# One level of Strassen for the down projection, with weight sums made in DRAM by accumulating transfers

## The chip, the cores and the metric

The program runs on one core of a Trainium2 chip. The metric is the device time of one execution in microseconds, taken as the median of several runs. A profile is one further look at an execution: it lists every instruction of each engine with its start and duration, and the DMA traffic. Engines are named as the profile names them: PE is TensorE, PEld its weight loads, DVE is VectorE, ACT is ScalarE, POOL is GpSimd, SP is SyncE (here it only issues DMAs).

## The reference

One decoder layer on 512 tokens of width 2048, in float32. It is a token mixer (gated linear attention, HGRN2 and latent attention head groups with one input and one output projection) followed by a SwiGLU feed-forward network of inner width 5632. Only the last line of the network is changed:

```python
x = x + rms_norm(m, attn_post_norm[l])
u = rms_norm(x, ffn_pre_norm[l])
f = (jax.nn.silu(u @ w_gate[l]) * (u @ w_up[l])) @ w_down[l]
x = x + rms_norm(f, ffn_post_norm[l])
```

Here `silu(...) * (...)` is 512 x 5632, called h below, and `w_down` is 5632 x 2048.

## The kernel before

Each float32 product is made of three matmuls. An operand is split into a high part, rounded to the type fp32r, and a low part, the remainder: `whi` (ACT, line 100) and `wlo` (DVE, line 107) split a weight tile, `split` (lines 128 and 129) an activation. `mm3` then issues high times high, high times low and low times high into one PSUM accumulator.

The stages follow one another. The mixer reads its weights as tiles of 128 x 1024 (512 KB) through `wsplit`: SP issues the load, ACT and DVE split it, PE works 24 matmuls of 512 columns on it. The tags `ws` (raw), `wh` and `wl` (split) have three buffers each, so SP runs a few tiles ahead of PE and waits until a buffer comes free. The first loops are `first_blocks` (eight tiles: four steps over the width of x, two blocks each) and two further blocks in `gemm_fm` (eight tiles). A scheduler that runs when the kernel is built sets the order of the instructions on each engine here; what a queue then does first is fixed.

After that `bridge` writes the order out by hand for PE, DVE, ACT and POOL: a list of `items` (a source tile, and the product that uses it), and dictionaries `pre_`, `post` and `tops` of functions that are called at an item's index. It contains the output projection, the norms, and gate and up. Gate and up already use one level of Strassen's scheme (Winograd's form, 7 products in place of 8): the weight differences are made by DVE (`tdiff`, line 1024). The first 24 of 44 units have two of their products done ahead (`NPRE`), and there POOL makes 256 of 1024 columns of the low part (line 109). SP's order is still the scheduler's.

`down` (line 1185) is the last stage. h has been written to DRAM by `hout` (`hd`, 44 tiles of 128 x 512). For each of two halves p of the output columns and each of 44 tiles k it loads one weight tile `wd[p, k]`, splits it and the h tile, and issues 24 matmuls of 512 columns (4 token groups x 2 column blocks x 3) into eight PSUM accumulators, 2 x 44 x 24 = 2112 in all:

```python
for tt in range(NTT):
    for c in range(2):
        self.mm3(ps[tt][c], hh[:, ts], hl[:, ts], wh[:, cs], wl[:, cs], k == 0, k == FT - 1)
```

The last six tiles of the second half are ordered by token group, so that three of the four groups are finished (squares, norm, residual, output) while PE still works.

## Time and profile before

| | |
|---|---|
| three timed runs | 2244.81, 2245.75 and 2250.26 us, median 2245.75 us |
| span of the profiled execution | 2249.2 us, 35218 instructions |
| PE busy | 2213.9 us, 98% |
| DVE / ACT / POOL busy | 1457.8 / 911.3 / 254.0 us |
| DMA moved | 299.86 MB, mean 133 GB/s |
| down projection | from about 1760 us to the end |

The span runs from the first to the last instruction; the profile gives no other time for that execution, and its span lies within the three timed runs. A row of a timeline gives the start, the duration, the engine, the line of the kernel, the operation, and what is written and read; in brackets is how long the engine was idle before it and what ended that. Matmuls overlap, so their pace is read from the distance of the starts and not from the duration.

### The profile page before, as it was taken

Reading aid. Unit: us, or ns where it says so; the run is one execution under the profiler, and the core shown is the slowest. Engines: PE = TensorE matmul, PEld = TensorE weight load, DVE = VectorE, ACT = ScalarE, POOL = GpSimd, SP = SyncE. Lnnn points to the kernel's source line nnn. Section 1 sums busy time; section 2 is a strip of 40 time slices with the busy share of each in tenths; the row PEclk is TensorE's granted clock in tenths of the full one; section 3 lists DMA queues with packets and bytes.
Section 4 is the critical chain, followed back from the end, with each engine's and each line's share of the span. In section 5 each row is a group of like instructions: output and inputs, shape, how many; then the busy total and the mean of one; then the engine's idle time right before and its main releaser. Section 6 shows DMA issues by size and latency. Waiting matters only on the chain.

```text
span 2249.2 us, 35218 instructions
## 1 busy us (share of the span) xinstructions
PE 2213.9 (98%) x14150; PEld 2005.5 (89%) x14150; DVE 1457.8 (65%) x2238; ACT 911.3 (41%) x1274; POOL 254.0 (11%) x218
## 2 busy tenths in 40 slices
PE   9999999999999999999999999999999999999998
PEld 7878887888879999999999999999999888888886
DVE  6347777535554577897888778999999623343345
ACT  5324343336553444654444444444343422232231
POOL 2012311000001665530000000000000000000000
PEclk9999899999999999999999999999999999999999
DMA  6222112232103576884333343666655744433332
GB/s 206 93 85 66 57 57 62 94 95 83 66 29 103 183 221 196 251 259 129 118 118 114 119 125 122 186 203 207 188 181 171 253 141 123 130 94 95 102 103 104
DMA packets 108340, 299.86 MB, mean 133 GB/s; under 512 B 12160, under 2 KB 29328, under 8 KB 108176
## 3 DMA queue, kind: packets, MB, share of 16 engines
q1 hardware_dynamic: 105152, 292.10, 41.6%
q10 hardware_dynamic: 3024, 5.51, 0.7%
q8 instruction: 111, 1.82, 0.3%
q14 instruction: 53, 0.43, 0.1%
HBM read 271.34 MB, written 26.21 MB: 132 GB/s over the span
## 4 chain that ended last, share of the span: by engine, by line
PE 90%; DVE 5%; POOL 1%; ACT 1%; issue 1%; DMA 1%; SPq 0%; DVEq 0%; ACTq 0%; POOLq 0%
PE acc L120 18%; PE acc L122 18%; PE acc L121 18%; PE aux L122 10%; PE aux L120 10%; PE aux L121 10%; DVE wl L107 1%; PE aux L541 1%; PE aux L755 1%; DVE u L526 1%; ACT wh L100 0%; DVE u L955 0%; PE aux L588 0%; PE aux L723 0%; PE aux L741 0%
## 5 line engine op out<-in xcount | busy, mean ns | idle before, releaser
L120 PE MATMUL acc<-u,wh 128*128 128x256 f32 (+2 forms) x2064 | 635.0, 309 | 2.6 <-ACT wh L270 1.4
L121 PE MATMUL acc<-u,wh 128*128 128x256 f32 (+2 forms) x2064 | 635.7, 308 | 0.0
L122 PE MATMUL acc<-u,wl 128*128 128x256 f32 (+2 forms) x2064 | 634.6, 308 | 0.1
L107 DVE TENSOR_TENSOR wl<-ws,wh 128x1024 fp32r<-128x1024 f32 (+2 forms) x315 | 375.5, 1193 | 305.2 <-ACT wh L100 299.0
L100 ACT ACTIVATE wh<-ws 128x1024 fp32r<-128x1024 f32 (+1 forms) x315 | 329.9, 1049 | 498.9 <-PE acc L121 141.2
L120 PEld LDWEIGHTS acc<-u,wh 128*128 128x128 f32 (+1 forms) x2064 | 395.5, 192 | 21.4 <-ACT wh L270 1.9
L122 PEld LDWEIGHTS acc<-u,wl 128*128 128x128 f32 (+1 forms) x2064 | 395.4, 192 | 19.1 <-DVE wl L107 1.0
L121 PEld LDWEIGHTS acc<-u,wh 128*128 128x128 f32 (+1 forms) x2064 | 395.8, 192 | 17.9 <-DVE u L250 0.4
L122 PE MATMUL aux<-u,wl 128*128 128x256 f32 (+1 forms) x1264 | 362.3, 287 | 1.9 <-DVE wl L107 1.9
L120 PE MATMUL aux<-u,wh 128*128 128x256 f32 (+1 forms) x1264 | 362.8, 287 | 0.3 <-ACT wh L100 0.3
L121 PE MATMUL aux<-u,wh 128*128 128x256 f32 (+1 forms) x1264 | 362.1, 286 | 0.0
L100 ACT ACTIVATE wh<-wt 128x1024 fp32r<-128x1024 f32 x176 | 186.9, 1062 | 299.1 <-PE aux L121 112.8
L122 PEld LDWEIGHTS aux<-u,wl 128*128 128x128 f32 x1264 | 243.5, 193 | 3.8 <-DVE wl L107 2.5
L120 PEld LDWEIGHTS aux<-u,wh 128*128 128x128 f32 x1264 | 243.6, 193 | 1.8 <-ACT wh L100 0.5
L121 PEld LDWEIGHTS aux<-u,wh 128*128 128x128 f32 x1264 | 243.6, 193 | 1.2
L107 DVE TENSOR_TENSOR wl<-wt,wh 128x1024 fp32r<-128x1024 f32 x176 | 215.0, 1222 | 34.0 <-ACT wh L100 33.9
L120 PE MATMUL acc<-wh,u 128*128 128x512 f32 x356 | 140.2, 395 | 0.0
L121 PE MATMUL acc<-wl,u 128*128 128x512 f32 x356 | 140.1, 394 | 0.0
L122 PE MATMUL acc<-wh,u 128*128 128x512 f32 x356 | 139.5, 394 | 0.0
L120 PE MATMUL acc<-wh,m 128*128 128x512 f32 x260 | 101.1, 389 | 0.0
L121 PE MATMUL acc<-wl,m 128*128 128x512 f32 x260 | 101.1, 389 | 0.0
L122 PE MATMUL acc<-wh,m 128*128 128x512 f32 x260 | 101.1, 389 | 0.0
(293 smaller groups left out, 3037.2 us busy)
## 6 DMA issues: line engine op xcount, KB each, us to landing
ws<-wgu_in SPq DMA_DIRECT2D x136, 512.0 KB, 3.8
wsx<-wgu_in SPq DMA_DIRECT2D x88, 512.0 KB, 3.7
ws<-wd_in SPq DMA_DIRECT2D x88, 512.0 KB, 3.7
ws<-wo_in SPq DMA_DIRECT2D x56, 512.0 KB, 3.7
ws<-wf_in SPq DMA_DIRECT2D x39, 512.0 KB, 3.6
ws<-wt_in SPq DMA_DIRECT2D x32, 512.0 KB, 3.6
hd<-g SPq DMA_DIRECT2D x44, 256.0 KB, 2.8
u<-hd SPq DMA_DIRECT2D x30, 256.0 KB, 3.9
```

What stands on the lines that cost most here:

```text
L100: self.nc.scalar.activation(h, st, AF.Copy)
L107: nc.vector.tensor_tensor(lo[:, :d], st[:, :d], h[:, :d], op=ALU.subtract)
L120: mm(ps, lhsT=ah, rhs=bh, start=start, stop=False)
L121: mm(ps, lhsT=ah, rhs=bl, start=False, stop=False)
L122: mm(ps, lhsT=al, rhs=bh, start=False, stop=stop)
L526: nc.vector.tensor_tensor(qt[hs].rearrange("p (c h n s) -> p c h n s", c=NTT, h=2, s=s)[:, :, h], c3(v3(q)[:, :, 1, :]), c3(dv[:, :, 1, :] ...
L541: mm(ps[:m, c * 64:(c + 1) * 64], lhsT=kt[:, c * P:c * P + m], rhs=qt[:, c * 64:(c + 1) * 64], start=True, stop=True)
L755: mm(po[:, ts], lhsT=v[kt][:, (h % 4) * P:(h % 4 + 1) * P], rhs=pT[:, kt * P:(kt + 1) * P], start=kt == 0, stop=kt == tt)
```

## The change

The down projection becomes one level of the same seven-product scheme. The inner width is cut into 11 groups of four tiles ("duos"), the tokens into two halves, the output columns into two halves; each weight block is cut again into 512-column parts p. An item is one 128 x 1024 tile of a weight block or weight sum, and has 12 matmuls of 512 columns (2 token groups x 2 tiles x 3). There are 2 parts x 11 duos x 7 products = 154 items and 1848 matmuls.

The four sums of weight blocks (td, 11.5 MB each) are not made by an engine. `weight_sums` copies a block of `wd` into `td` in DRAM with eight plain transfers on SP's queue (1.44 MB each), and then adds another block with eight accumulating transfers on POOL's queue. There are 32 plain and 32 accumulating transfers: t1 and t3 are copied (16), both get b12 added (16), t2 is copied from t1 (8), gets b22 (8), t4 is copied from t2 (8), gets b21 (8). The program calls one step of it at every second weight tile of the mixer, 40 in all, and the other 24 at units of gate and up.

The sums of h blocks are made by DVE, products are gathered in two PSUM pairs that are evacuated after each product into 16 accumulators in SBUF, and the stage joins the hand-written list, so that its loads may begin seven items ahead. The last norm and the output are in `stat` and `final`.

```diff
--- before.py
+++ after.py
-NEXT = 22
...
+NROW = DFF * D // 4 // 2048
...
+    def weight_sums(self):
+        nc, t = self.nc, self.t
+        flat = lambda v: v.rearrange("a d p n -> (a d p n)").rearrange("(r n) -> r n", n=2048)
+        b11, b12, b21, b22 = (flat(t["wd"][q]) for q in range(4))
+        t1, t2, t3, t4 = (flat(t["td"][q]) for q in range(4))
+        for step in (((t1, b11, False), (t3, b22, False)), ((t1, b12, True), (t3, b12, True)),
+                     ((t2, t1, False),), ((t2, b22, True),), ((t4, t2, False),),
+                     ((t4, b21, True),)):
+            for dst, src, add in step:
+                for r in range(0, NROW, NROW // 8):
+                    d, v = dst[r:r + NROW // 8], src[r:r + NROW // 8]
+                    if add:
+                        nc.gpsimd.dma_start(d, v, accum_op=ALU.add, max_dma_last_dim=8192)
+                    else:
+                        nc.sync.dma_start(d, v)
+                    yield
+
     def wsplit(self, src, n=1024):
+        if self.bg is not None:
+            self.nbg += 1
+            if self.nbg % 2 == 0 and self.nbg <= 80:
+                next(self.bg, 0)
...
-        with tc.tile_pool(name="ext", bufs=NEXT, reuse_waits="tile") as self.M:
-            self.down()
...
         self.first_blocks(wf, scaled(hf))
+        self.bg = self.weight_sums()
...
+            at(pre_, i, lambda: next(self.bg, 0))
+        self.down_items(items, pre_, post, tops, at)
...
-    def down(self):
+    def down_items(self, items, pre_, post, tops, at):
         nc, t = self.nc, self.t
-        hs = []
-
-        def load(k):
-            h = self.u() if k < NHU else self.mx()
-            nc.sync.dma_start(h, t["hd"][k])
-            hs.append(h)
-
-        for k in range(4):
-            load(k)
-        gr, x2 = [], {}
-
-        def loads():
+        base = len(items)
+        duos = [NPRE + 4 * d for d in range((FT - NPRE) // 4)] + [4 * d for d in range(NPRE // 4)]
+        chunks = [duos[i:i + 2] for i in range(0, len(duos), 2)]
+        nchunk = len(chunks)
...
+        def sload(d):
+            r = raw[d] = {}
+            for n, e, hs in (("11", 0, 0), ("21", 0, 256), ("22", 1, 256), ("12", 1, 0)):
+                r[n] = self.u()
+                nc.sync.dma_start(
+                    r[n].rearrange("p (k s) -> p k s", k=2),
+                    t["hd"][d + e:d + 4:2].rearrange("k p s -> p k s")[:, :, hs:hs + 256])
+
+        def ssum13(d):
+            r = raw[d]
+            r["S1"] = self.u()
+            D.tensor_tensor(r["S1"], r["21"], r["22"], op=ALU.subtract)
+            D.tensor_tensor(r["21"], r["11"], r["21"], op=ALU.subtract)
+            r["S3"] = r.pop("21")
...
+        def conv(d, kind):
+            S[d, kind] = self.split(raw[d][KEY[kind]])
+        ORDER = (1, 5, 6, 3, 7, 2, 4)
...
+        def load(i, p, n, d):
+            tag = TAGS[i % 10]
...
+            q = SRC[n]
+            nc.sync.dma_start(st, (t["wd"][q] if q < 4 else t["td"][q - 4])[p, duos.index(d)])
...
+        def prod(c, p, n, d):
...
+                for tt in range(2):
+                    for j in range(2):
+                        a = slice(j * 256 + tt * P, j * 256 + (tt + 1) * P)
+                        w = slice(j * 512, (j + 1) * 512)
+                        mm = lambda l, r, st, sp: nc.tensor.matmul(
+                            ps[tt], lhsT=l[:, a], rhs=r[:, w], start=st, stop=sp,
+                            skip_group_check=True)
+                        mm(hi, wh, first and j == 0, False)
+                        mm(hi, wl, False, False)
+                        mm(lo, wh, False, last and j == 1)
...
+        def evac(c, p, n):
+            ps = bank[which(p, n)]
+            name, sign = EV[n]
+            for tt in range(2):
+                a = acc.get((p, name, tt))
+                if a is None:
+                    a = acc[p, name, tt] = self.u()
+                    nc.scalar.activation(a, ps[tt], AF.Copy, scale=float(sign))
+                elif sign > 0:
+                    D.tensor_tensor(a, a, ps[tt], op=ALU.add)
+                else:
+                    D.tensor_tensor(a, a, ps[tt], op=ALU.subtract)
...
+        def stat(p, name, tt, eng=None):
...
+            if name == "C11":
+                D.tensor_tensor(f, bank[p][tt], f, op=ALU.add)
+            sq = self.gv()
+            nc.scalar.activation(sq, f, AF.Square, accum_out=ssc[tok][:, cc:cc + 1])
+            (eng or D).tensor_tensor(f, f, gr[cc], op=ALU.mult)
+
+        def final(tok):
+            ss = self.sm(1)
+            D.reduce_sum(ss, ssc[tok], axis=mybir.AxisListType.X)
+            r = self.rstd(ss, D_, 1)
+            row, tt = tok // 2, tok % 2
+            for cc in range(4):
+                f = acc[cc % 2, f"C{row + 1}{cc // 2 + 1}", tt]
+                D.scalar_tensor_tensor(f, f, r, x2[tok, cc], op0=ALU.mult, op1=ALU.add)
+                nc.sync.dma_start(self.out[tok * P:(tok + 1) * P, cc * 512:(cc + 1) * 512], f)
...
+        for c, ds in enumerate(chunks):
+            for p in range(2):
+                b0 = len(items)
+                for o, n in enumerate(ORDER):
+                    for k, d in enumerate(ds):
+                        i = len(items)
+                        j = i - base
+                        at(pre_, max(base - 4, i - 7), load, j, p, n, d)
+                        items.append((lambda j=j: W.pop(j), prod(c, p, n, d), 0))
+                    if n in EV:
+                        at(pre_, len(items), evac, c, p, n)
...
+        for name, o in (("C12", -2), ("C22", -1), ("C11", 0)):
+            for tt in range(2):
+                at(pre_, end + o, stat, 1, name, tt)
+        for tok in (0, 1):
+            at(pre_, end, final, tok)
+        for tt in range(2):
+            at(pre_, end + 1, stat, 1, "C21", tt, D)
+        for tok in (2, 3):
+            at(pre_, end + 1, final, tok)
...
     a["wd"] = np.ascontiguousarray(
-        f["w_down"][0].reshape(FT, P, 2, 1024).transpose(2, 0, 1, 3))
+        f["w_down"][0].reshape(FT // 4, 2, 2, P, 2, 2, 512)[[k // 4 for k in order]]
+        .transpose(2, 4, 5, 0, 3, 1, 6)).reshape(4, 2, FT // 4, P, 1024)
...
+                     ("td", (4, 2, FT // 4, P, 1024))):
```

The order on SP after the 16 loads of x and the small constants, before the change. `ws_...` is a weight tile in the order of use; `ws_355` is the sixth of the sixteen tiles named above.

```order
L95 DMA ws_355<-wf_in 128x1024
L95 DMA ws_417<-wf_in 128x1024
L95 DMA ws_447<-wf_in 128x1024
L95 DMA ws_524<-wf_in 128x1024
L95 DMA ws_554<-wf_in 128x1024
L95 DMA ws_584<-wf_in 128x1024
L95 DMA ws_614<-wf_in 128x1024
L95 DMA ws_652<-wf_in 128x1024
L95 DMA ws_682<-wf_in 128x1024
```

The same place after the change (a tile may have another number: 555 is 554 before, 585 is 584, 616 is 614, 654 is 652, 685 is 682). `td<-wd_in` is a plain copy of 1.44 MB, `td<-td` one that reads a finished t1.

```order
L126 DMA td<-wd_in 32x11264 x2
L95 DMA ws_355<-wf_in 128x1024
L126 DMA td<-wd_in 32x11264 x5
L95 DMA ws_417<-wf_in 128x1024
L126 DMA td<-wd_in 32x11264 x4
L95 DMA ws_447<-wf_in 128x1024
L126 DMA td<-wd_in 32x11264 x5
L95 DMA ws_524<-wf_in 128x1024
...
L126 DMA td<-td 32x11264 x2
L95 DMA ws_616<-wf_in 128x1024
L126 DMA td<-td 32x11264 x5
L95 DMA ws_654<-wf_in 128x1024
L126 DMA td<-td 32x11264
L95 DMA ws_685<-wf_in 128x1024
```

All 24 plain copies of the mixer's share now stand among these eight loads, the first two ahead of `ws_355` and the last just ahead of `ws_685`, the fourteenth tile.

POOL before, behind its last sum of squares of x (`m_104`); line 515 is the decay product of the first head groups. In brackets are the counters that a row waits for.

```order
L258 TENSOR_TENSOR m_104<-m_104,m_361 128x512 [waits DVE_49,Activation_49]
L258 TENSOR_TENSOR m_104<-m_104,m_377 128x512 [waits DVE_49,Activation_49]
L515 TENSOR_TENSOR m_1084<-u_508,m_1086 128x512 [waits Activation_49,Pool_49]
L515 TENSOR_TENSOR m_1106<-u_510,m_1108 128x512 [waits Activation_49]
L515 TENSOR_TENSOR m_1085<-u_508,m_1121 128x512 [waits Activation_49]
```

POOL after the change at the same place. `DMAHW0` to `DMAHW7` count finished transfers of SP's queue, `DMASW0` to `DMASW7` those of POOL's; line 535 is line 515 of before.

```order
L277 TENSOR_TENSOR m_104<-m_104,m_377 128x512 [waits DVE_49,Activation_49]
L124 DMA td<-wd_in 176x2048 [waits DMAHW6_49]
L124 DMA td<-wd_in 176x2048 [waits DMAHW7_49]
...
L124 DMA td<-wd_in 176x2048 [waits DMAHW7_49]
L124 DMA td<-wd_in 176x2048 [waits DMAHW0_49,DMASW0_49]
...
L124 DMA td<-wd_in 176x2048 [waits DMAHW0_49,DMASW7_49]
L535 TENSOR_TENSOR m_1092<-u_508,m_1094 128x512 [waits Activation_49,Pool_49]
```

Each of the 16 accumulating transfers waits for the plain copy that it adds to, and the second eight also for the first eight. All of them now stand ahead of the head groups' work on POOL.

SP before, where gate and up reach the third of the full units; `ws` and `wsx` are its weight tiles, `wsx_10043` the last of them.

```order
L1042 DMA wsx_9808<-wgu_in 128x1024 [waits DMAHW3_49,DVE_49]
L95 DMA ws_10039<-wgu_in 128x1024 [waits DMAHW4_49,DVE_49,Activation_49]
L1042 DMA wsx_10041<-wgu_in 128x1024 [waits DMAHW5_49,DVE_49]
L95 DMA ws_10077<-wgu_in 128x1024 [waits DMAHW6_49,DVE_49]
L1042 DMA wsx_10043<-wgu_in 128x1024 [waits DMAHW7_49,DVE_49]
L1098 DMA hd<-g_9839 128x512 [waits DMAHW0_49,DVE_49]
```

SP after the change; `wsx_10084` is `wsx_10043` of before.

```order
L1062 DMA wsx_9848<-wgu_in 128x1024 [waits DMAHW3_49,DVE_49]
L126 DMA td<-td 32x11264 [waits DMAHW4_49,DMASW0_49]
L95 DMA ws_10080<-wgu_in 128x1024 [waits DMAHW5_49,DVE_49,Activation_49]
L126 DMA td<-td 32x11264 [waits DMAHW6_49,DMASW1_49]
L1062 DMA wsx_10082<-wgu_in 128x1024 [waits DMAHW7_49,DVE_49]
L126 DMA td<-td 32x11264 [waits DMAHW0_49,DMASW2_49]
L95 DMA ws_10118<-wgu_in 128x1024 [waits DMAHW1_49,DVE_49]
...
L126 DMA td<-td 32x11264 [waits DMAHW6_49,DMASW7_49]
L1062 DMA wsx_10084<-wgu_in 128x1024 [waits DMAHW7_49,DVE_49]
L1118 DMA hd<-g_9879 128x512 [waits DMAHW0_49,DVE_49]
```

Eight copies of t2 into t4 stand among that unit's four loads, and each waits for an accumulating transfer of POOL (`DMASW0` to `DMASW7`), which POOL issues behind its last low part (line 109).

## Rows read from the trace of the kernel before

**Rows 1.** The page, part 1 with its head: busy us, share of span, instructions.

```profile
span 2249.2 us, 35218 instructions
PE 2213.9 (98%) x14150; PEld 2005.5 (89%) x14150; DVE 1457.8 (65%) x2238; ACT 911.3 (41%) x1274; POOL 254.0 (11%) x218
```

**Rows 2.** Windows of four stretches; columns as in the first line.

```profile
core 0: us, PE busy (x) PEld busy (x) DVE busy (x) ACT busy (x) POOL busy (x), PEclk, DMA share, GB/s
0.00:100.00 100.00, 94.84 (x406) 76.69 (x407) 56.43 (x85) 50.61 (x75) 12.76 (x12) 0.98 0.48 160
1500.00:1600.00 100.00, 100.00 (x836) 100.00 (x835) 93.91 (x117) 42.82 (x47) 0.00 (x0) 1.00 0.63 197
1800.00:2200.00 400.00, 400.00 (x1767) 331.31 (x1766) 141.43 (x152) 119.44 (x161) 0.00 (x0) 1.00 0.39 115
2200.00:2249.00 49.00, 39.59 (x175) 32.48 (x173) 26.28 (x84) 6.53 (x18) 0.00 (x0) 0.95 0.23 86
```

**Rows 3.** Timeline of the TensorE, 39 to 46.5 us: start, us, operation.

```profile
39.91 1.05 PE L190 MATMUL aux<-one,m 128*128 128x1 f32 x8 [1.06 <-DVE m L258]
...
42.43 0.63 PE L120 MATMUL acc<-u,wh 128*128 128x512 f32 x1
...
44.56 0.63 PE L122 MATMUL acc<-u,wl 128*128 128x512 f32 x1
44.99 0.63 PE L120 MATMUL acc<-u,wh 128*128 128x512 f32 x1
...
45.93 0.39 PE L120 MATMUL acc<-u,wh 128*128 128x512 f32 x1
46.16 0.39 PE L121 MATMUL acc<-u,wh 128*128 128x512 f32 x1
```

**Rows 4.** Timeline of the SP queue's DMA issues, 15 to 120 us.

```profile
21.68 0.34 SPq L313 DMA_DIRECT2D w<-w_in  x1
23.04 48.48 SPq L95 DMA_DIRECT2D ws<-wf_in  x11
```

**Rows 5.** DMA issues of the first 30 us: KB each, median us to landing.

```profile
m<-xT_in SPq DMA_DIRECT2D x16, 256.0 KB, 6.5
ws<-wf_in SPq DMA_DIRECT2D x7, 512.0 KB, 6.5
```

**Rows 6.** The page, part 6: the same kind of load over the whole run.

```profile
ws<-wf_in SPq DMA_DIRECT2D x39, 512.0 KB, 3.6
```

**Rows 7.** Windows of short stretches; last columns: granted clock, DMA share, GB/s.

```profile
10.00:15.00 5.00, 3.78 (x15) 2.23 (x14) 2.60 (x4) 3.41 (x6) 1.34 (x1) 1.00 1.03 401
985.00:1000.00 15.00, 15.00 (x128) 15.00 (x127) 14.93 (x29) 9.40 (x18) 4.84 (x6) 1.00 0.80 233
```

**Rows 8.** Timeline of GpSimd around 1005 us, its last work.

```profile
1004.50 1.51 POOL L109 TENSOR_TENSOR wl<-ws,wh 128x256 fp32r<-128x256 f32 x1 [1.31 <-ACT wh L100]
```

**Rows 9.** Timeline of the SP queue, 1015 to 1041 us.

```profile
1033.81 0.33 SPq L1042 DMA_DIRECT2D wsx<-wgu_in  x1
```

**Rows 10.** Timeline of the VectorE, 1047 to 1056 us.

```profile
1049.90 1.22 DVE L1024 TENSOR_TENSOR wt<-wsx,wt 128x1024 f32<-128x1024 f32 x1
```

**Rows 11.** Lines by form, 1770 us to the end: count, busy us, mean ns, idle before.

```profile
L107 DVE TENSOR_TENSOR wl<-ws,wh 128x1024 fp32r<-128x1024 f32 x79 | 96.8, 1226 | 105.8 <-ACT wh L100 105.8
L129 DVE TENSOR_TENSOR m<-u,m 128x512 fp32r<-128x512 f32 x42 | 28.6, 692 | 105.6 <-ACT m L128 102.6 <-PE aux L121 3.0
L1216 DVE TENSOR_TENSOR u<-aux,u 128x512 f32<-128x512 f32 x8 | 5.5, 687 | 0.0
```

**Rows 12.** Timeline of all engines, the last 10 us.

```profile
2239.21 0.39 PE L122 MATMUL aux<-u,m 128*128 128x512 f32 x1
...
2240.96 0.15 DVE L1253 TENSOR_REDUCE sm<-ssc 128x1 f32<-128x4 f32 x1
...
2243.46 2.74 DVE L1256 SCALAR_TENSOR_TENSOR u<-u,sm,u 128x512 f32<-128x512 f32 x4
2244.24 2.32 SPq L1258 DMA_DIRECT2D out_y<-u  x4
```

More of the change, by code (lines that the diff above doesn't have):

```diff
@@ L69, in __init__ @@
         self.uid = 0
+        self.bg = None
+        self.nbg = 0
     def nm(self, s):
@@ new lines, in which, with f @@
+        def which(p, n):
+            return p if n == 2 else "ab"[p ^ (n in (5, 3))]
+        def prod(c, p, n, d):
+            def f(wh, wl):
+                if (c, p, n) == (0, 0, 1) and d == chunks[0][0]:
+                    bank["a"] = [self.acc(), self.acc()]
+                    bank["b"] = [self.acc(), self.acc()]
+                if c == 0 and n == 2 and d == chunks[0][0]:
+                    bank[p] = [self.aux(), self.aux()]
+                ps = bank[which(p, n)]
+                hi, lo = S[d, KIND[n]]
+                first = d == chunks[c][0] and (n in (1, 5) or (n == 2 and c == 0))
+                last = d == chunks[c][-1]
+                for tt in range(2):
[8 more added lines that the diff above has]
+                        mm(lo, wh, False, last and j == 1)
+            return f
@@ new lines, in down_items @@
+        EV = {1: ("C11", 1), 5: ("C22", 1), 6: ("C12", -1), 3: ("C12", 1), 7: ("C22", -1),
+              4: ("C21", 1)}
+        def evac(c, p, n):
+            ps = bank[which(p, n)]
+            name, sign = EV[n]
[6 more added lines that the diff above has]
+                    D.tensor_tensor(a, a, ps[tt], op=ALU.add)
+                else:
+                    D.tensor_tensor(a, a, ps[tt], op=ALU.subtract)
@@ new lines, in tail_loads @@
+        def tail_loads():
+            for i in range(4):
+                gr[i] = self.u()
+                nc.sync.dma_start(gr[i], t["grow"][:, i * 512:(i + 1) * 512].broadcast_to([P, 512]))
+            for tt in range(4):
+                for cc in range(4):
+                    x2[tt, cc] = self.u()
+                    nc.sync.dma_start(x2[tt, cc], t["x2d"][tt, cc])
+        def stat(p, name, tt, eng=None):
+            f = acc[p, name, tt]
+            row, col = int(name[1]) - 1, int(name[2]) - 1
+            tok, cc = 2 * row + tt, 2 * col + p
+            if tok not in ssc:
+                ssc[tok] = self.C.tile([P, 4], F32, name=f"ssc{tok}")
+            if name == "C11":
[3 more added lines that the diff above has]
+            (eng or D).tensor_tensor(f, f, gr[cc], op=ALU.mult)
@@ new lines, in down_items @@
+        end = len(items)
+        at(pre_, end - 9, tail_loads)
+        for k, name in enumerate(("C12", "C22", "C11", "C21")):
+            for tt in range(2):
+                at(pre_, end - 6 + k, stat, 0, name, tt)
+        for name, o in (("C12", -2), ("C22", -1), ("C11", 0)):
[3 more added lines that the diff above has]
+            at(pre_, end, final, tok)
+        for tt in range(2):
+            at(pre_, end + 1, stat, 1, "C21", tt, D)
```

109 lines of the change are left out of this document (50 added, 59 removed).

## The prediction

> **What bounds the kernel now.** I read the page's first part, then the windows by stage, then the two places where the order moves. PE is busy 98% of a span of 2249.2 us [rows 1], and from 1500 to 2200 us it never rests, with DVE at 94% in gate and up and at 35% in the down projection [rows 2]. In the down projection a matmul starts every 400 / 1767 = 0.226 us (some records may be missing); the starts in the early stage, 0.23 us apart, agree [rows 2, 3]. So PE sets the time from end to end, and a matmul less is worth 0.227 us if nothing else gets in its way. The change takes matmuls out of the last stage and puts transfers into earlier ones, so the question is what those transfers make PE wait for. The DMA engines are not idle there: in the first 30 us they are the limit. At 10 to 15 us they move 401 GB/s at a share of 1.03, and loads that land in 3.6 us over the whole run (512 KB) take 6.5 us while others stand before them in the queue; even the 256 KB loads of x take 6.5 us [rows 5 to 7]. So I take a queue as served in order: a load pays for what stands ahead of it.
>
> **The matmuls removed.** 2112 become 1848, 264 less: 264 x 0.227 = 59.9 us gained.
>
> **The tail.** PE's last matmul starts at 2239.2 us; behind it stand one evacuation, one norm chain of 2.5 us (2240.96 to 2243.46), four fused multiply-adds in 2.74 us and the last output, 9.6 us from PE's end to the end of the span [rows 12]. Now the four token groups end together. Behind the last product DVE has, in its order, two additions, the C11 block (four operations), two norm chains with eight multiply-adds, two more multiplications, and again two chains with eight. By the same rows that is 8 x 0.69 + 4 x 2.5 + 4 x 2.74 = 26.5 us, then 3 us for the last output [rows 11, 12]: about 29.5 us in place of 9.6, so 20 us lost.
>
> **The engines in the down projection.** Per chunk of 28 items DVE has 28 low parts (1.23 us), 14 low parts of activations, 8 sums and 24 evacuations (0.69 us each) [rows 11]: 34 + 32 = 66 us, in 28 x 12 x 0.227 = 76 us of PE. That is 87%, and PE never waited at 94% [rows 2]. I put 5 us for uneven stretches, bounds 0 and 15. The loads ask for 154 x 0.52 MB in 420 us, 192 GB/s, with the h tiles (44 x 0.26 MB) 220, a little over half of what the queue has shown [rows 7].
>
> **The transfers: what one costs.** A plain copy of 1.44 MB has no row. If it goes as fast as the fastest stretch of loads, 400 GB/s, it takes 3.6 us of all 16 engines; if its reading and its writing of DRAM cost as much as a load and a store one after the other, 7.2 us [rows 7]. The stretch with many small stores among the loads (985 to 1000 us) moves 233 GB/s at a share of 0.80, so 290 at full share, 5.0 us for a copy [rows 7]. Both ends of a copy are in DRAM, so I take a value above that: 6.2 us. An accumulating transfer reads once more. Its bounds are 3.6 us (as a copy) and 10.8 us (three legs), and I take one and a half copies, 9.3 us. Both kinds share the 16 engines with the weight loads. The Trainium skill, page "DMA: Bandwidth & Descriptors", section "Latency and other measured facts", gives 207 to 214 GB/s for copies between tensors in HBM whose pitch does no harm; by it a copy is an estimated 6.8 us and the whole sum some 2560 us. No run here shows it yet.
>
> **The first stall, in the mixer.** After the change SP issues the 24 copies among eight weight loads, the first two at about 21.7 us [rows 4], and five of them stand between one load and the next, where PE has 5.45 us of work (24 x 0.227) per load. PE reaches the fourteenth tile (`ws_685` after) at 82 us: 328 matmuls stand ahead of it in PE's order, and 406 are done at 100 us, so 78 x 0.227 before that [rows 2]. SP runs ahead of PE by three buffers, some 16 us of PE's work. Ahead of this load the queue must now pass 24 copies and 9 loads (512 KB at 400 GB/s, 1.31 us each), and the t2 copies wait for the first 8 accumulating transfers on POOL's queue, which run on the same engines; part of the other 8 is served in the meantime, I take 4. Together 24 x 6.2 + 12 x 9.3 + 9 x 1.31 = 272 us, from 21.7 us, and 2.3 us to split the tile: 296, against 82. PE stalls 214 us. Cheap end: 24 x 3.6 + 8 x 3.6 + 12 = 127, a stall of 69 us. Dear end: 24 x 7.2 + 16 x 10.8 + 12 = 357, a stall of 299 us. The head groups' products wait on POOL behind the 16 accumulating transfers, but no longer than PE waits for these tiles. Nothing takes the time back: PE has 5 us of idle time in this stretch [rows 2].
>
> **The second stall, in gate and up.** POOL's last work ends at 1006.0 us [rows 8]; the eight transfers that add b22 to t2 follow at once. SP stands at a copy of t2 that waits for each of them, with the loads of the third unit in between. The last of these loads is issued at 1033.8 us now, and DVE needs its tile at 1049.9 [rows 9, 10]. After the change it stands behind 8 accumulating transfers, 8 copies and 3 loads: 8 x (9.3 + 6.2) + 4 x 1.31 = 129 us after 1006, so at 1135, 85 us late, and DVE and PE with it. Bounds 19 us (8 x 7.2) and 105 us (8 x 18). The last eight additions, b21 into t4, hold nobody up: td is read only by the down projection, some 600 us later.
>
> **The clock.** Behind a wait of 1.06 us at 39.9 us PE's starts were 0.43 us apart, its lower level (1.2 GHz), and 0.23 us again from 45.9 on; the nine starts from 42.43 to 45.93 took 3.5 us in place of 2.0, 1.5 us lost [rows 3]. Eight waits of this kind cost 12 us, bounds 5 and 20.
>
> **Sum**, against the profiled span: 2249.2 - 59.9 + 20 + 5 + 12 + 214 + 85 = 2525 us. With all cheap ends (0, 5, 69 and 19 for the last four) 2302, with all dear ends (15, 20, 299 and 105) 2648. The span is 3.5 us above the median of the runs (2245.75 us) and within them, less than the price of one copy; I leave it out.
>
> **Rivals.** (1) The transfers stay hidden, and the kernel is faster: 2249.2 - 59.9 + 20 + 5 = 2214 us. For it speaks a DMA share of 0.48 in the first 100 us and 0.63 at 1500 to 1600 us [rows 2]. Against it: the 24 copies would have to pass in the 46 us between 21.7 and 80 us that the nine loads leave, 1.9 us each, or 750 GB/s, with the additions for nothing; the best stretch is 401. It decides from there. (2) Adding in the transfer is much dearer than moving: nothing in the trace excludes 20 us each. Then the first eight alone hold the t2 copies: 24 x 6.2 + 8 x 20 + 12 gives a stall of 263 us, more if some of the second eight are served first, and the second stall is 8 x 26.2 + 5 after 1006, 171 us: with 2226 for the other terms 2226 + 263 + 171 = 2660 us and up to 2760. (3) Weight loads overtake the copies in the engines, so that only the waits written into SP's order remain: the fourteenth tile's load stands behind the wait for the eighth addition, 21.7 + 8 x (6.2 + 9.3) = 146 us, a stall of 66; with the second stall 2226 + 66 + 85 = 2377 us. Against it stands the 6.5 us of the early loads [rows 5]. The Trainium skill's same page, section "Issuing engines are not separate DMA queues", says that transfers started by different engines run on the same 16 DMA engines and interleave; by that POOL's queue adds no bandwidth, as in the sum. The runs of before have no transfer of POOL's to compare.
>
> **The chances.** The two stalls as summed: 0.75, its own range 2302 to 2648. Rival (2): 0.12. Rival (3): 0.08. Rival (1): 0.05. The predicted time is the first case's. The range 2300 to 2680 leaves out rival (1), most of rival (2) and little else. Within 0.3% (7 us) a measurement of this kernel can't be told from no change; faster than that has rival (1)'s 0.05, the same 0.01, slower 0.94.
>
> **What would show it.** In the changed profile: PE idle in the first 300 us, in steps, with the releaser a split of a mixer tile and behind it a load; SP waiting for transfers of POOL; DMA share near 1 there; a second gap of PE between about 1050 and 1135 us plus the first delay; then a down projection about 60 us shorter with no waits, and a tail of some 30 us. The prediction is wrong if weight tiles land in 4 us although copies stand before them, if a copy takes less than 3 us, or if the down projection waits for DVE.

## The result, and the profile after

The changed kernel takes 2428.85 us (median of 4 runs, 2425.46 to 2428.97) against 2246.28 us on the same chip: a ratio of 1.0806, 95% interval 1.0790 to 1.0821. It is 8% slower; 2525 us were predicted, with a range of 2300 to 2680.

First the head of the page and its slices of the span (60.7 us each), beside [rows 1]:

```profile
span 2427.0 us, 35385 instructions
PE 2176.2 (90%) x13886; PEld 1969.2 (81%) x13886; DVE 1626.4 (67%) x2463; ACT 985.0 (41%) x1341; POOL 282.1 (12%) x250
PE   6246999999999999999538999999999999999994
PEclk8677999999999999999768999999999999999997
DMA  9999422122221356789996433355556577677662
q0 software_dynamic: 6144, 46.14, 9.5%
```

PE has 264 matmuls less and is idle in two places, and where it is idlest the DMA row reads 9. q0 is POOL's queue; its columns are packets, MB and share of 16 engines. By it one accumulating transfer takes 0.095 x 2427.0 / 32 = 7.2 us of all engines.

The windows of the two places and of the new down projection, beside [rows 2]:

```profile
0.00:100.00 100.00, 48.95 (x192) 38.84 (x192) 39.60 (x67) 34.60 (x57) 21.55 (x23) 0.76 1.00 312
100.00:200.00 100.00, 40.77 (x160) 31.82 (x160) 19.41 (x27) 13.51 (x16) 8.70 (x8) 0.67 1.01 285
1100.00:1200.00 100.00, 77.75 (x603) 77.14 (x602) 55.61 (x81) 32.80 (x45) 20.08 (x19) 0.86 0.97 262
1200.00:1300.00 100.00, 46.22 (x321) 44.93 (x320) 34.79 (x41) 17.13 (x19) 5.13 (x6) 0.68 0.99 263
2000.00:2200.00 200.00, 200.00 (x884) 165.58 (x883) 155.06 (x185) 102.43 (x122) 0.00 (x0) 1.00 0.68 216
```

The chain that ended last names what PE stood for (start, duration, what; only its longest pieces are listed):

```profile
38.94 48.53 DMA td<-wd_in
87.53 48.94 DMA ws<-wf_in
139.26 33.55 DMA td<-td
172.88 49.12 DMA ws<-wf_in
...
1146.04 43.38 DMA ws<-wgu_in
...
1206.95 41.97 DMA wsx<-wgu_in
1252.87 27.14 DMA wsx<-wgu_in
```

A 512 KB load that took 6.5 us in the busiest stretch of before [rows 5] takes 49 us. The DMA issues from 20 to 220 us (count, KB each, median us to landing) show it for all:

```profile
td<-wd_in SPq DMA_DIRECT2D x16, 1408.0 KB, 44.9
td<-wd_in POOLq DMA_DIRECT2D x16, 1408.0 KB, 90.9
td<-td SPq DMA_DIRECT2D x8, 1408.0 KB, 44.5
ws<-wf_in SPq DMA_DIRECT2D x11, 512.0 KB, 48.0
```

Four marks split the difference of the two spans, 177.8 us. Two rows of the changed kernel, and one of before:

```profile
1124.53 1.51 POOL L109 TENSOR_TENSOR wl<-ws,wh 128x256 fp32r<-128x256 f32 x1 [1.25 <-ACT wh L100]
1971.26 0.40 PE L1284 MATMUL acc<-wh,u 128*128 128x512 f32 x1
```

```profile
1758.03 0.40 PE L120 MATMUL acc<-wh,u 128*128 128x512 f32 x1
```

GpSimd's last low part starts at 1124.53 us, against 1004.50 [rows 8]; the first matmul of the down projection starts at 1971.26, against 1758.03; the last at 2395.97, against 2239.21 [rows 12]; the span ends at 2427.0, against 2249.2. So: first stall +120.0, second stall +93.2, down projection 424.7 in place of 481.2 us, -56.5, and the end from the last matmul's start 31.0 in place of 10.0, +21.0.

The end (VectorE, and the last outputs of SP), beside [rows 12]: four times a norm chain with four multiply-adds, where before one stood behind PE's end.

```profile
2395.97 0.39 PE L1284 MATMUL acc<-wh,u 128*128 128x512 f32 x1
...
2404.11 2.74 DVE L1336 SCALAR_TENSOR_TENSOR u<-u,sm,u 128x512 f32<-128x512 f32 x4
2404.89 18.98 SPq L1337 DMA_DIRECT2D out_y<-u  x16
...
2420.76 2.74 DVE L1336 SCALAR_TENSOR_TENSOR u<-u,sm,u 128x512 f32<-128x512 f32 x4
```

### The profile page after: what moved, and what is told of

It reads as the page before. It is cut to its first block, busy times and chain, and to the rows that moved or that the text cites. A ratio compares the mean times of both kernels' runs of the same rounds, so it can differ in the third digit from the quotient of the medians.

```text
span 2427.0 us, 35385 instructions
## 1 busy us (share of the span) xinstructions
PE 2176.2 (90%) x13886; PEld 1969.2 (81%) x13886; DVE 1626.4 (67%) x2463; ACT 985.0 (41%) x1341; POOL 282.1 (12%) x250
## 3 DMA queue, kind: packets, MB, share of 16 engines
q0 software_dynamic: 6144, 46.14, 9.5%
## 4 chain that ended last, share of the span: by engine, by line
PE 74%; DMA 15%; DVE 6%; POOL 1%; issue 1%; ACT 1%; another core or an unknown queue 1%; SPq 0%; DVEq 0%; ACTq 0%; POOLq 0%
PE acc L1284 14%; PE acc L143 12%; PE acc L141 12%; PE acc L142 12%; PE aux L143 6%; PE aux L141 6%; PE aux L142 6%; DMA ws<-wf_in 4%; DMA wsx<-wgu_in 3%; DMA td<-wd_in 3%; PE aux L1284 2%; DMA ws<-wgu_in 2%; DMA td<-td 1%; DVE wl L107 1%
## 5 line engine op out<-in xcount | busy, mean ns | idle before, releaser
L141 PE MATMUL acc<-u,wh 128*128 128x256 f32 (+2 forms) x2064 | 643.6, 313 | 107.3 <-ACT wh L100 104.8
L107 DVE TENSOR_TENSOR wl<-ws,wh 128x1024 fp32r<-128x1024 f32 (+2 forms) x279 | 334.0, 1198 | 345.1 <-ACT wh L100 342.0
L100 ACT ACTIVATE wh<-ws 128x1024 fp32r<-128x1024 f32 (+1 forms) x279 | 292.5, 1050 | 573.2 <-DMA ws<-wf_in 122.6
L100 ACT ACTIVATE wh<-wt 128x1024 fp32r<-128x1024 f32 x238 | 252.5, 1061 | 440.8 <-PE aux L142 108.2
L1284 PE MATMUL acc<-wh,u 128*128 128x512 f32 x1056 | 327.6, 389 | 1.7 <-DVE u L1306 1.7
L107 DVE TENSOR_TENSOR wl<-wt,wh 128x1024 fp32r<-128x1024 f32 x238 | 290.3, 1220 | 49.9 <-ACT wh L100 48.3
L1284 PEld LDWEIGHTS acc<-wh,u 128*128 128x128 f32 x1056 | 198.2, 188 | 43.6 <-issue 2.5
L1284 PE MATMUL acc<-wl,u 128*128 128x512 f32 x528 | 205.4, 389 | 0.0
L100 ACT ACTIVATE wh<-wsx 128x1024 fp32r<-128x1024 f32 x90 | 95.6, 1062 | 126.8 <-issue 44.2
L107 DVE TENSOR_TENSOR wl<-wsx,wh 128x1024 fp32r<-128x1024 f32 x90 | 109.8, 1220 | 20.1 <-ACT wh L100 18.6
L1284 PEld LDWEIGHTS acc<-wl,u 128*128 128x128 f32 x528 | 99.1, 188 | 20.5
```

Source lines behind the costliest of these rows:

```text
L100: self.nc.scalar.activation(h, st, AF.Copy)
L107: nc.vector.tensor_tensor(lo[:, :d], st[:, :d], h[:, :d], op=ALU.subtract)
L141: mm(ps, lhsT=ah, rhs=bh, start=start, stop=False)
L1284: mm = lambda l, r, st, sp: nc.tensor.matmul(ps[tt], lhsT=l[:, a], rhs=r[:, w], start=st, stop=sp, skip_group_check=True)
```

## The experiments

Theory: the loss is two stalls, and each comes from weight loads that stand in SP's queue behind bunched copies, which in turn share the engines with POOL's additions or wait for them. Rivals: the traffic itself wherever it stands, the price of an accumulating transfer, the written waits alone, the new down projection. Single runs are given without an interval.

**Without the sums.**

```diff
-        self.bg = self.weight_sums()
+        self.bg = iter(())
-            nc.sync.dma_start(st, (t["wd"][q] if q < 4 else t["td"][q - 4])[p, duos.index(d)])
+            nc.sync.dma_start(st, t["wd"][q % 4][p, duos.index(d)])
```

> No transfer into td is issued; the down projection reads blocks of wd in place of the sums, so the four sums are left out of what is computed. Everything else is as in the changed kernel. Theory (both stalls come from the transfers): the trace of the changed kernel places about 120 us of delay before 1005 us and 90 us between 1110 and 1310 us; without them 2427 - 210 = 2217 us, 2210 to 2225. Rival (part of the loss is the new down projection or its place in the hand-written list): above 2235 us. Rival (weight reads of the sums are slow because td was written late): below 2210 us.

Measured: 2213.66 us, ratio 0.9848 (0.9833 to 0.9862), profiled span 2214.3. Its down projection runs from 1758.02 to 2183.87 us. So all of the loss, and more, is the transfers; the new down projection is out as a cause. The prediction's sum without the stalls was 2214.

**Copies alone.**

```diff
-                    if add:
-                        nc.gpsimd.dma_start(d, v, accum_op=ALU.add, max_dma_last_dim=8192)
-                    else:
+                    if not add:
                         nc.sync.dma_start(d, v)
-                    yield
+                        yield
```

> The 32 accumulating transfers are left out, the 32 plain copies stay (td then holds copies and no sums). In the changed kernel SP's queue took 56.4% of the engines from 20 to 220 us; less twelve loads of 1.31 us that is (113 - 16) / 24 = 4.0 us a copy. Theory (a load waits for what stands ahead of it in SP's queue): 24 x 4.0 + 9 x 1.31 = 108 us from 21.7 us, so the fourteenth tile is split at 132 us, against 82: a stall of 50 us; in gate and up eight copies of 4.0 us without waits, 0 to 20 us. About 2277 us, 2255 to 2300. Rival (loads overtake copies, only waits for POOL's transfers hold SP up): 2217 us, the same as without sums. Rival (the copies are the cost and the additions ride along): above 2350 us.

Measured: 2302.61 us. The expectation missed by 25 us, and the time lies just above its range, since leaving the additions out also moved the eight copies into t4 forward: 32 copies stand among the mixer's loads, and gate and up have none. Windows of that kernel, columns as in [rows 2]:

```profile
50.00:100.00 50.00, 15.00 (x48) 11.42 (x48) 12.14 (x16) 10.89 (x16) 0.00 (x0) 0.64 1.00 341
100.00:150.00 50.00, 24.65 (x85) 19.03 (x86) 4.90 (x4) 5.51 (x5) 0.00 (x0) 0.72 1.00 354
1100.00:1200.00 100.00, 100.00 (x836) 100.00 (x835) 80.15 (x96) 42.30 (x46) 0.00 (x0) 1.00 0.41 129
```

At 341 to 354 GB/s a copy of 1.44 MB takes 4.2 us. 32 x 4.2 + 9 x 1.31 = 146 us from 21.5 us on, less 82 and with 2.3 us for the split, is a stall of 88 us; the span is 86.5 us longer than without sums. The sum agrees better than its parts do: the load of the fourteenth tile, issued at 145.47 us, lands 27.4 us later, at 172.9, where the formula has 168; that would be a stall of 93, of which some is made good further on. The copies alone, with no addition to wait for, make that stall: loads do not overtake them.

**Additions as plain copies on the same queue.**

```diff
-                        nc.gpsimd.dma_start(d, v, accum_op=ALU.add, max_dma_last_dim=8192)
+                        nc.gpsimd.dma_start(d, v, max_dma_last_dim=8192)
```

> The 32 accumulating transfers become plain copies of the same bytes on the same queue of POOL, in the same order with the same waits (td then holds one block, no sums). In the changed kernel one accumulating transfer took 0.095 x 2427 / 32 = 7.2 us of all 16 engines, a plain copy 4.0 us. Theory (engine time ahead of the loads is the price): each of the 16 transfers of the mixer is 3.2 us cheaper, so the first stall falls by 40 to 50 us and the second, with 8 such transfers ahead of the load and 8 beside it, by 25 to 45: about 2350 us, 2320 to 2370. Rival (the written waits between SP and POOL are the price, whatever a transfer takes): within 20 us of the changed kernel. Rival (accumulating is dear in a way of its own, copies are cheap): below 2300 us.

Measured: 2346.44 us, as the theory had it.

```profile
q0 software_dynamic: 6144, 46.14, 5.4%
```

By this share 0.054 x 2344.7 / 32 = 4.0 us for a transfer: an accumulating one costs 1.8 times as much. GpSimd's last low part starts at 1087.32 us (1001.04 without sums), so the first stall is 86 us, and the rest of the 130 us, 44, is the second. By the same marks the changed kernel has 123 and 89, so the first fell by 37 us, a little less than expected, and the second by 45.

**The program's order kept.**

```diff
-                        nc.gpsimd.dma_start(d, v, accum_op=ALU.add, max_dma_last_dim=8192)
+                        i = nc.gpsimd.dma_start(d, v, accum_op=ALU.add, max_dma_last_dim=8192)
                     else:
-                        nc.sync.dma_start(d, v)
+                        i = nc.sync.dma_start(d, v)
+                    self.tc.keep_in_program_order(i)
```

> All 64 transfers stay, each is only kept behind what the program has issued on its engine before it, so that SP's queue has one copy behind every second weight tile (32 tiles for the first 16 copies) and one per unit in gate and up; the result is the full one. Theory (the bunch of copies ahead of a few loads is what stalls PE): 24 x 4.0 + 16 x 7.2 = 211 us of all engines are spread over some 600 us in which the loads leave the engines idle for about 70% of the time; the stalls fall to 0 to 20 us in all, about 2225 us, 2215 to 2240, faster than before. Rival (total traffic, not its place, is the price): above 2300 us. Rival (the wait of SP for POOL's additions only moves to a later tile): 2260 to 2350 us with a new stall where the t2 copies stand.

Measured: 2248.57 us (10 runs, 2236.95 to 2251.11), ratio 0.9995 (0.9981 to 1.0009). The same 64 transfers of the same bytes now cost 33 us and not 213: place, and not traffic, is the price. But 33 us were left where 0 to 20 were expected. From 900 to 1300 us PE's waits (total, count, longest) have one of 17.6 us for a low part:

```profile
PE acc L144 <- DVE wl L107: 17.6, 1, 17.6
```

GpSimd's timeline shows why:

```profile
1011.62 7.03 POOL L124 DMA_DIRECT2D td<-wd_in  x8
1207.65 0.85 POOL L124 DMA_DIRECT2D td<-wd_in  x1 [189.00 <-DMA td<-td]
```

POOL has nothing else to do and issues its eight additions at once. The DMA part for 1011 to 1070 us:

```profile
q0 software_dynamic: 1281, 9.71, 79.0%
q1 hardware_dynamic: 2032, 5.42, 24.8%
...
ws<-wgu_in SPq DMA_DIRECT2D x5, 512.0 KB, 24.6
wsx<-wgu_in SPq DMA_DIRECT2D x4, 512.0 KB, 28.5
```

No copy stands ahead of these loads (SP's copies into t4 come later; the first addition to one waits 189 us), and they still take 25 to 28 us in place of 3.6. The window begins before POOL's transfers do, so SP's queue has more packets in it; from 1018 to 1068 us, with work in both queues, the counts are 1185 for q0 and 1186 for q1.

**Order kept in the mixer only.** (`gateup` is set to true where `bridge` begins.)

```diff
+                    if not self.gateup:
+                        self.tc.keep_in_program_order(i)
```

> Only the 40 transfers of the mixer are kept in the program's order; the 24 of gate and up stay as in the changed kernel, with eight copies in front of one unit's loads, each waiting for an addition of POOL. The result is the full one. Theory (two separate stalls): the first one falls to the 8 or 9 us that the ordered kernel showed by 1008 us (2008 against 1001 without sums), the second stays at the 89 us that the changed kernel lost between 1124 us and the down projection: 2214 + 9 + 89 = 2312 us, 2295 to 2330. Rival (the second stall is a consequence of the first, since its additions meet a delayed unit): below 2280 us.

Measured: 2310.99 us, 1 us from the expectation (whose 2008 should read 1008): the two stalls are separate, and add up.

**All transfers on POOL's queue.**

```diff
-                        nc.sync.dma_start(d, v)
+                        nc.gpsimd.dma_start(d, v, max_dma_last_dim=8192)
```

> All 64 transfers are issued by POOL, the plain ones too; SP's queue holds loads alone. POOL's order is the scheduler's: 40 transfers stand ahead of the first head groups' products, and the sums of squares of x stand among the additions. The result is the full one. Theory (a load waits for what stands ahead in its own queue, and otherwise only shares the engines): the weight loads of the first 200 us land in 6 to 12 us instead of 48, and the wait moves to POOL: 16 x 4.2 + 3 x 7.2 = 89 us from 8 us on before the sums of squares go on (PE needs them at 39), and 24 x 4.2 + 16 x 7.2 = 216 us before the head groups (PE needs them at about 100). About 2214 + 130 for these, and 0 to 40 for the 24 transfers of gate and up that share the engines with loads: 2345 us, 2290 to 2400. Rival (the engines are simply full and the queue does not matter): weight loads land in 30 us or more there, 2400 us or more. Rival (another queue hides it): below 2240 us.

Measured: 2399.16 us, at the upper end, and neither side was right. The weight loads of 20 to 220 us took 16.9 us, not 6 to 12, and the loads of x 31.4, though no copy stood ahead of them in SP's queue. The DMA part for 20 to 60 us:

```profile
q0 software_dynamic: 1479, 11.12, 76.9%
q1 hardware_dynamic: 1478, 3.09, 23.3%
```

The two queues moved the same number of packets. Those of x hold 2 KB, POOL's 8 KB. In the changed kernel it was 784 and 790 packets from 60 to 130 us. By the Trainium skill, page "DMA: Bandwidth & Descriptors", section "Queues, rings and completion order", each engine goes round the queues that have work, a packet at a time; these counts agree. This made a new theory: beside POOL's transfers a load pays one of their packets for each of its own.

**POOL's additions paced by PE.** Each waits for the last matmul that the program issued ahead of it. The edit is shown against the ordered kernel.

```diff
                         i = nc.gpsimd.dma_start(d, v, accum_op=ALU.add, max_dma_last_dim=8192)
+                        self.behind_matmul(i)
                     else:
                         i = nc.sync.dma_start(d, v)
-                    self.tc.keep_in_program_order(i)
+                        self.tc.keep_in_program_order(i)
...
+        pe = next(x for x in reversed(self.nc.cur_bb.bb.instructions)
+                  if x.engine == mybir.EngineType.PE)
+        self.tc.add_manual_dep(i.ins, pe.name, mybir.DependencyInfo(
+            mybir.DependencyClass.Sync, mybir.DependencyReason.DATA), reason="paced")
```

> As the ordered kernel, and each accumulating transfer of POOL also waits for the last matmul that the program issued ahead of it, so that they start one per two weight tiles (mixer) or one per unit (gate and up) as far as POOL's order allows. The result is the full one. Theory (what was left, 33 us over the kernel without sums, is the eight additions that POOL issued within 7 us at 1011 us, 58 us of engine time beside loads that need half of it, with a wait of 17.6 us, and 15 bunched ones at 430 us): 2214 + 10 = 2224 us, 2215 to 2235, faster than before. Rival (the traffic itself costs it wherever it stands): 2240 to 2250 us, as the ordered kernel. Rival (POOL's waits for PE delay its own products for the head groups): above 2250 us.

Measured: 2221.39 us, ratio 0.9890 (0.9869 to 0.9911). The 17.6 us are gone, and all 64 transfers cost 8 us against the kernel without sums.

**The ordered kernel with small packets.**

```diff
-                        i = nc.gpsimd.dma_start(d, v, accum_op=ALU.add, max_dma_last_dim=8192)
+                        i = nc.gpsimd.dma_start(d, v, accum_op=ALU.add, max_dma_last_dim=2048)
```

> The ordered kernel, with each accumulating transfer cut into packets of 2 KB in place of 8 KB; bytes, order and result are the same. In the changed kernel SP's queue and POOL's moved nearly the same number of packets while both had work (784 and 790 from 60 to 130 us, 747 and 736 from 130 to 180 us), a packet of a load holding 4 KB and one of an addition 8 KB. Theory (the engines take packets of the two queues in turn, so a load beside an addition waits for one of its packets for each of its own): with 8 KB packets an engine takes 7.2 x 16 / 176 = 0.65 us for each, so a load of 8 packets per engine takes 8 x (0.65 + 0.16) = 6.5 us; with 2 KB some 2.6 to 4 us. The wait of 17.6 us at 1030 to 1060 us falls below 6 us, and the time to about 2235 us, 2225 to 2242. Rival (shares go by bytes or by engine time): no change, 2240 to 2252 us. Rival (small packets make an addition much dearer in all): above 2255 us, and q0's share well above 10.2%.

Measured: 2219.25 us, ratio 0.9872 (0.9854 to 0.9889), better than expected, and against the ordered kernel 29 us from one number. Its DMA part for 1011 to 1070 us, beside the one above:

```profile
q0 software_dynamic: 3892, 7.81, 71.5%
q1 hardware_dynamic: 2775, 8.00, 37.7%
...
ws<-wgu_in SPq DMA_DIRECT2D x6, 512.0 KB, 7.6
wsx<-wgu_in SPq DMA_DIRECT2D x6, 512.0 KB, 7.0
```

A load takes 7 us beside the same eight additions. The theory's pace of 6.5 us for a load with 8 KB packets was not the time to landing: the ordered kernel's loads took 25 to 28 us, as several stand in SP's queue at once. The counts are no longer equal, since SP's queue now gets what its loads ask for: it moves 8.00 MB in these 59 us, and the whole kernel without sums 7.03 MB. The additions are dearer in engine time, not cheaper: q0's share of the whole span is 11.6%, 0.116 x 2219.3 / 32 = 8.0 us each. So shares go by packets; the rival of shares by bytes or by engine time is out.

**All on POOL's queue, small packets.** The same number in the kernel with POOL's queue alone.

> The kernel with all 64 transfers on POOL's queue, their packets 2 KB in place of 8 KB; the result is the full one. In that kernel, from 20 to 60 us, POOL's queue moved 1479 packets and SP's 1478, but 11.12 MB against 3.09 MB, and the loads of x took 31.4 us (median of 8). Theory (packets in turn): x has packets of 2 KB, so each load of x shares half and half in bytes; its median falls to about 15 us (12 to 20), PE's early waits shrink by 20 to 40 us, and POOL's transfers take correspondingly longer while loads stand beside them. Rival (shares by bytes or time): the loads of x still take 27 us or more.

Measured: 2318.95 us, 80 us less than with 8 KB. From 20 to 60 us:

```profile
q0 software_dynamic: 2576, 10.09, 67.9%
q1 hardware_dynamic: 2550, 5.09, 34.1%
...
m<-xT_in SPq DMA_DIRECT2D x7, 256.0 KB, 18.4
```

One to one again, and the loads of x fall from 31.4 to 18.4 us. In bytes it is still two to one: over the whole run q0 has 34816 packets, 11776 more than the ordered kernel with small packets (23040), for 32 plain transfers. In 8 KB packets a transfer has 6144 / 32 = 192 packets, 16 more than its 176 pieces; without these 16 the plain ones have 11264 for 46.14 MB, or 4 KB each. The plain transfers, which POOL issues in this stretch, were cut to 4 KB only, twice the packets of x.

**Small packets in the changed kernel.** The same number, order as in the change.

> The changed kernel with one number changed: the packets of its accumulating transfers hold 2 KB in place of 8 KB. Order, waits, bytes and result are the same. In the ordered kernel this took a load beside the additions from about 25 to 7 us. Theory (here the written order is the price: a load stands behind copies, and these behind POOL's additions, so that an addition's whole duration counts, 8.0 us with 2 KB packets against 7.2): no gain in the second stall, 89 us or up to 10 more; in the first SP's queue may pass its copies a little sooner and the t2 copies wait longer for the additions; 2400 to 2450 us. Rival (the 8 KB packets of the additions, taken in turn with SP's, are the price of both stalls): below 2370 us.

Measured: 2405.66 us, inside the range. GpSimd's last low part starts at 1117.44 us, 7 us sooner; the second stall is 16 us shorter, where none was expected. With this order the small packets give back 23 of 213 us; the order alone, with 8 KB packets, gives back 180 (the ordered kernel): the order is the main cause.

But the reason given for the first stall no longer holds here. The loads of 20 to 220 us land in 14.6 us in place of 48.0, and PE's waits for their tiles fall from 104.8 to 56.9 us (0 to 300 us). What takes their place is a wait for GpSimd:

```profile
PE aux L561 <- POOL m L535: 55.6, 3, 50.1
```

Line 535 makes the head groups' decay products, which stand in POOL's order behind the 16 additions; POOL issues the last of these at 193.97 us and makes the first product at 194.67. In the changed kernel the last addition went out at 166.54 and PE waited for POOL only 9.2 us. So two orders held PE there, SP's and POOL's, and the second lay close behind the first.

**Another end.** The paced kernel, with the norm chains of two groups joined, C11 earlier, and part of the last work on ACT and GpSimd.

```diff
-            r = self.rstd(ss, D_, 1)
+            r = self.rstd(ss, D_, 2)
...
+                if i % 4 == 0:
+                    nc.scalar.activation(f, f, AF.Copy, scale=r[:, tt:tt + 1])
+                    G.tensor_tensor(f, f, x2[tok, cc], op=ALU.add)
...
-        for name, o in (("C12", -2), ("C22", -1), ("C11", 0)):
+        for name, o in (("C12", -2), ("C22", -1), ("C11", -1)):
```

> As the paced kernel, with another end: the two token groups of a half share one norm chain, the C11 block is finished one item earlier, ahead of the last product, the squares and multiplications of C21 stand ahead of the first half's final multiply-adds, and four of the sixteen final ones go to ACT and GpSimd. The result is the full one. In the changed kernel the end took 30.6 us from PE's last matmul. Theory (DVE's work behind the last product is the tail): four chains of 2.5 us become two (5 us), C11 with its waits runs beside the last product (3 to 4 us), four multiply-adds leave DVE (2.7 us) and two multiplications too (1.4 us): 12 us less than the paced kernel, a tail of 18 us. Rival (the last outputs, issued 1.2 us apart by SP, are the tail): no more than 3 us less.

Measured: 2217.56 us, ratio 0.9876 (0.9852 to 0.9899); from PE's last matmul (2184.19) to the end 29.1 us against 31.1 in the paced kernel. The expectation of 12 us failed; in time the two kernels can't be told apart, as their intervals overlap. VectorE and GpSimd there:

```profile
2190.22 2.48 POOL L1335 TENSOR_TENSOR u<-u,u 128x512 f32<-128x512 f32 x2 [721.11 <-ACT g L1334]
2190.22 1.28 DVE L199 TENSOR_SCALAR sm<-sm 128x2 int32<-128x2 int32 x1
2191.54 1.19 DVE L201 TENSOR_SCALAR sm<-sm 128x2 int32<-128x2 int32 x1
...
2194.52 6.08 DVE L1348 SCALAR_TENSOR_TENSOR u<-u,sm,u 128x512 f32<-128x512 f32 x6
```

Two operations of 0.17 us last 1.28 and 1.19 us beside GpSimd, and a multiply-add 1.01 us in place of 0.68: what GpSimd took over, VectorE paid in waiting.

**The end without GpSimd.**

```diff
-                for o, n in enumerate(ORDER):
+                for o, n in enumerate(ORDER if (c, p) != (nchunk - 1, 1) else (1, 5, 6, 3, 2, 7, 4)):
...
+        for name, o in (("C11", -2), ("C12", -2), ("C22", 0), ("C21", 0)):
+            at(pre_, end + o, stat, 1, name)
+            if name == "C12":
+                at(pre_, end - 1, final, 0)
+        at(pre_, end + 1, final, 1)
```

> The paced kernel with an end that uses no GpSimd: in the last seven products the one for C11 (n = 2) moves ahead of 7 and 4, so that the first token half is complete 24 matmuls (5.4 us) before PE's end; additions, squares and multiplications of a block stand in pairs; the two groups of a half share one norm chain. The result is the full one. The first try at the end gained 2 us only: behind PE's end DVE still had all of C11 (it was late already), six multiply-adds took 6.08 us in place of 4.1 while GpSimd worked beside it, and two operations of the norm chain 1.2 us in place of 0.17. Theory (DVE's backlog and GpSimd's share of DVE's time are what kept it): from the end of the product for C11 DVE has 26 us of work, 5.4 of it before PE's end, and 2.3 us for the last output: a tail of 23 us against 31, so about 2213 us, 2209 to 2217. Rival (the outputs or ACT's squares bound the tail): no better than the first try, 2216 us or more.

Measured: 2212.63 us, ratio 0.9847 (0.9831 to 0.9862), the fastest kernel of the study with the full result. 2213 was expected, but the split is another: the end is 19 us, and PE ends 5.5 us later than in the paced kernel, since its last product now waits for the evacuation of C22, which VectorE does late (a wait of 5.4 us on a `u` of line 1314). Multiply-adds take 0.67 us again:

```profile
2192.95 0.39 PE L1292 MATMUL acc<-wh,u 128*128 128x512 f32 x1
...
2203.20 5.39 DVE L1348 SCALAR_TENSOR_TENSOR u<-u,sm,u 128x512 f32<-128x512 f32 x8
```

## Why the prediction was right, and where it was not

The direction, the mechanism and the places were right: two stalls, at the copies among the mixer's loads and at the third unit of gate and up. The time was 96 us too long, and most of that is one term.

- **Matmuls and unevenness** (-59.9 + 5): -56.5. 884 matmuls in 200 us are 0.226 us each, and unevenness cost 3.4 us of the 5 (bounds 0 and 15); PE's waits for VectorE, busy at 78%, come to 4.9 us there.
- **The end** (+20): +21.0, as worked out from the rows of before.
- **The first stall** (+214): +120. The step that failed is the price of a transfer. A copy takes 4.2 us, not 6.2 (bounds 3.6 to 7.2), an accumulating one 7.2, not 9.3. With these the same formula gives 24 x 4.2 + 12 x 7.2 + 9 x 1.31 = 199 us from 21.7 us, 221. The load of the fourteenth tile is the first of three that SP issues behind the last copy (rows of SP's and of PE's timeline):

```profile
167.22 38.67 SPq L95 DMA_DIRECT2D ws<-wf_in  x3
...
216.39 0.50 PE L141 MATMUL acc<-u,wh 128*128 128x512 f32 x1 [3.25 <-ACT wh L100]
```

It lands 48.0 us after its issue, at 215.2, and PE starts on the tile at 216.39 (the chain's load that lands at 172.88 + 49.12 = 222.0 is the next tile's). From 20 to 220 us q0 moved 17.34 MB, twelve transfers of 1.44 MB, as many as were counted. So queue order and count were right. By the figure of the Trainium skill that the prediction weighed (page "DMA: Bandwidth & Descriptors", section "Latency and other measured facts", 207 to 214 GB/s) a copy came to an estimated 6.8 us; the runs measure 341 to 354 GB/s, and the measurement decides.
- **"Nothing takes the time back"**: wrong by some 20 us. SP's next eight loads (`ws<-wt_in`) start at 217.62 us against 73.17 without sums, 144 us late; at 1124 us it is 123 against the same kernel. Of the small matmuls of the head groups (line 561), which stood between large products before, 42 now run ahead of 243 us, where the last of these waits ends, but they take only 7 us. The rest of the cause stays open.
- **The second stall** (+85): +93, for partly wrong reasons. With the measured prices the formula gives 8 x (7.2 + 4.2) + 4 x 1.31 = 96 us after 1126, 1222, where the tile was needed at 1049.9 + 120 = 1170: 52 us. The last of that unit's loads, issued at 1206.95, lands at 1248.9, 27 us after the 1222, and the load at 1252.87 takes another 27.14. Beside them runs what the prediction put at nothing: "The last eight additions, b21 into t4, hold nobody up". POOL starts the first of these at 1183.01 us and the last at 1242.60:

```profile
1183.01 0.85 POOL L124 DMA_DIRECT2D td<-wd_in  x1 [49.98 <-DMA td<-td]
```

By the packets in turn a load then pays for each of its own packets. This is read from these rows; no run leaves out these eight alone. That 85 came near 93 is luck: two errors of opposite sign met.
- **The clock** (+12): not to be separated. In 1100 to 1300 us a matmul takes 123.97 / 921 = 0.135 us of PE's time, without sums 200.00 / 1669 = 0.120, at granted clocks of 0.77 and 1.00: 14 us in that stall alone. But they lie within the stalls, where PE often waits for the next tile anyway, and are part of the 120 and 93.
- **The rivals.** (1), hidden transfers at 2214 us, is what the kernel without sums takes, and what the paced one comes close to; in this order it is out. (2) is out, an addition costs 7.2 us. (3), overtaking, is out: loads take 48 us, and copies alone stall PE by 86.

## What to carry to other kernels

A transfer that nothing waits for is cheap only if it is kept back (8 us for all 64 when paced, 213 us as scheduled): this scheduler moved it to the front of its queue, and every later load or product of that queue stood behind it. Write its place into the order (one per tile), and let the issue of background transfers on another queue wait for the work that they lie beside. Where two queues must share, cut the background's packets below the size of the loads' (2 KB beside 4 KB here); and price a transfer of a new kind by a run of its own before building on it.

## What the runs showed of the hardware

- Queues share the engines packet by packet (784 and 790, 1185 and 1186, 1479 and 1478, 2576 and 2550), so that loads of 4 KB packets beside additions of 8 KB packets took 25 to 28 us, several of them in the queue, and 7 us beside the same additions in 2 KB packets.
- A DRAM to DRAM copy of 1.44 MB takes 4.2 us of all engines, an accumulating transfer of that size 7.2 us in 8 KB packets and 8.0 us in 2 KB packets.
- VectorE slows beside GpSimd: 1.28 us for an operation of 0.17, 1.01 us for one of 0.68. The Trainium skill, page "Trainium Architecture — The Big Picture", section "What this means for kernel authors", says that the two share a port pair by an exclusive lock; these rows agree: the two slow operations fill the 2.48 us of GpSimd's two.
